# Residual rows of a hybrid layer: the store of h1 and h2 moved from right behind its accumulating DMA to a later step

## The chip, the cores and the metric

The kernel runs on one core of a Trainium2 chip. The metric is the device time of one execution in microseconds (us). Three runs of the kernel before took 2553.04, 2545.64 and 2548.37 us, a median of 2548.37 us.

## The reference

One layer of a transformer-like trunk over 2048 rows ("tokens") of 1024 float32 numbers:

```python
u = rms_norm(h, g_mix_pre[l]); z = u @ w_in[l]
ya = swa_with_sinks(...); yh = hgrn2(...)          # two head groups
y = jnp.concatenate([ya, yh], axis=-1) @ w_out[l]
h = h + rms_norm(y, g_mix_post[l])                 # h1
u = rms_norm(h, g_x_pre[l]); m = rms_norm(mem, g_mem[l])
y = cross_attention(u, m, wq_x[l], wk_x[l], wv_x[l], wo_x[l])
h = h + rms_norm(y, g_x_post[l])                   # h2
u = rms_norm(h, g_ffn_pre[l])
y = (jax.nn.silu(u @ w_gate[l]) * (u @ w_up[l])) @ w_down[l]
h = h + rms_norm(y, g_ffn_post[l])
```

The change concerns the two middle sums, h1 and h2: each is kept in DRAM for the sum that comes after it, and each is normalised at once for the product that follows.

## The kernel before

**Products.** Every float32 matrix is split into a high and a low part, and a product is three matmuls: high by high (line L1117), high by low (L1118), low by high (L1119). The high part comes from `split2` on ACT (L980, ScalarE) or POOL (L982, GpSimd), the low part on DVE (L983, VectorE). A split weight block is called T in the trace, a split block of activations S. Blocks of 2x2 are multiplied by a scheme with seven products (`seven`), whose sums of operands are formed on DVE (L1086).

**Stages around the change.** After the token mixing come, as steps of one long loop in `phases`: the out projection (`mixed_block`), the scores of cross attention (`score_block`), the values (`value_block`, whose weights hold the memory's values times the output matrix), and then the feed-forward blocks (`hidden_blocks`, `down_block`). A block of the first three works on two tiles of 128 rows, numbered n and n + 1; NT is 16, so each stage has eight blocks. A step is one of the seven products. After it `phases` advances every running generator by one `yield`: the `after()` of the blocks already computed, the splits and the loads of coming weights.

**After a block of the out projection.** `out` adds the partial products into a row tile y[i] (L1482 on DVE, L1484 on ACT) and has ACT square it (L1460). `after()` forms the inverse root of the mean square in three small POOL instructions (`rstds`, L1471 to L1475), scales the row (DVE, L1507), and starts on POOL a DMA that adds the input row onto it (`add`, L1489, an accumulating DMA). Right behind it stands the store of the row into `h1_d`. It is issued on SP (SyncE) and has to wait until the accumulating DMA has landed. Then `rest()` squares the finished row for the next norm (`mean_squares`, ACT, L1460), takes its `rstds`, transposes the row on PE (L1371) with copies on ACT (L1372), and stores it to `h1t_d`. Blocks n = 12 and 14 (n >= NT - 4) do not go on at once: their `rest()` is handed to the next stage and loads the row from DRAM again.

**After a block of the values** the same happens with `h2_d`: scaling at L1591, adding the row of `h1_d`, store into `h2_d`. Its `rest()` scales once more (L1612), transposes, stores to `u_d`, and for some blocks forms differences on DVE (L1627, L1628, L1631, L1632), stores them in quarters (`u_s0`) and first loads an earlier row of `u_d` for that purpose.

**What sets the order.** `load` (L75) and `store` (L78) both issue on SP, so they share one queue in which a waiting store holds up everything behind it. Row tiles come from one pool of nine (`row_tile`); who takes a tile next waits for the last reader of its earlier contents. The order of the instructions on each engine is not that of the text: a scheduler of the tile framework places them by a time simulation of its own. `with self.behind():` tells that scheduler that what follows may be placed only behind the last instructions of ACT, DVE, PE and SP that the step had; it adds no wait to the program.

Of the kernel before, what the change touches and what calls it, by code (L numbers as in the profile page):

```python
# [18 lines left out]
P = 128  # L19
# [10 lines left out]
NT = T // P  # L30
# [18 lines left out]
class Layer:  # L49
# [1441 lines left out]
    def mixed_block(self, n):  # L1491
        nc = self.nc
        y, ss = {}, []

        def out(i, j, a, b):
            if not y:
                ss.append(self.small("q_s", 4))
                if not n:
                    self.g_mix_post = self.gain(self.I["g_mix_post"])
            if i not in y:  # L1500
                y[i] = self.row_tile()
            self.squared(y[i][:, j * 512:(j + 1) * 512], a, b, ss[0][:, 2 * i + j:2 * i + j + 1])

        def after():
            r = self.rstds(ss[0])
            for i in range(2):
                nc.vector.scalar_tensor_tensor(y[i], y[i], r[:, i:i + 1], self.g_mix_post, ALU.mult, ALU.mult)  # L1507
                self.add(y[i], self.I["x"], n + i)
                self.store(self.h1_d[(n + i) * P:(n + i + 1) * P, :], y[i])
                yield  # L1510
            if n < NT - 4:
                yield
                yield from rest()

        def rest():
            s2 = self.small("q_s", 4)
            if n >= NT - 4:
                for i in range(2):
                    y[i] = self.rows_of(self.h1_d, n + i)
                for _ in range(3):  # L1520
                    yield
            for i in range(2):
                self.mean_squares(y[i], i, s2)
                yield
            r = self.rstds(s2)
            nc.gpsimd.tensor_scalar(self.r_x[:, n:n + 2], r, 1.0, None, ALU.mult)
            yield
            for i in range(2):
                self.store(self.h1t_d[n + i], self.transposed(y[i], y[i]))
                yield  # L1530

        if n >= NT - 4:
            self.rests[0].append(rest)

        return self.tokens(self.y_d, n), out, after, None

    def score_block(self, n):
# [35 lines left out]
    def value_block(self, n):  # L1573
        nc = self.nc
        y, ss = {}, []

        def out(i, j, a, b):
            if not y:
                ss.append(self.small("q_s", 4))
            if i not in y:  # L1580
                y[i] = self.row_tile()
                if n == 0 and len(y) == 1:
                    self.g_x_post = self.gain(self.I["g_x_post"])
                    self.g_ffn_pre = self.extra_tile()
                    self.load(self.g_ffn_pre, self.I["g_ffn_pre"][0:1, :].broadcast_to([P, D]))
            self.squared(y[i][:, j * 512:(j + 1) * 512], a, b, ss[0][:, 2 * i + j:2 * i + j + 1])

        def after():
            r = self.rstds(ss[0])
            for i in range(2):  # L1590
                nc.vector.scalar_tensor_tensor(y[i], y[i], r[:, i:i + 1], self.g_x_post, ALU.mult, ALU.mult)  # L1591
                self.add(y[i], self.h1_d, n + i)
                self.store(self.h2_d[(n + i) * P:(n + i + 1) * P, :], y[i])
                yield
            if n < NT - 4:
                yield
                yield from rest()

        def rest():
            s2 = self.small("q_s", 4)  # L1600
            if n >= NT - 4:
                for i in range(2):
                    y[i] = self.rows_of(self.h2_d, n + i)
                for _ in range(3):
                    yield
            for i in range(2):
                self.mean_squares(y[i], i, s2)
                yield
            r = self.rstds(s2)
            u = [self.row_tile() for _ in range(2)]  # L1610
            for i in range(2):
                nc.vector.scalar_tensor_tensor(u[i], y[i], r[:, i:i + 1], self.g_ffn_pre, ALU.mult, ALU.mult)  # L1612
                yield
            o = []
            yield
            for i in range(2):
                tv = self.transposed(u[i], u[i])
                self.store_transposed(self.u_d, n + i, tv)
                if 4 <= n < 8:
                    o.append(self.row_tile().rearrange("p (k t) -> p k t", k=KT))  # L1620
                    self.load(o[i], self.u_d[:, :, (n + i - 4) * P:(n + i - 3) * P].rearrange("k p t -> p k t"))
                yield
            for i in range(len(o)):
                tv = u[i].rearrange("p (k t) -> p k t", k=KT)
                s = self.row_tile().rearrange("p (k t) -> p k t", k=KT)
                with self.behind():
                    nc.vector.tensor_tensor(s[:, 0:4], tv[:, 0:4], o[i][:, 0:4], ALU.subtract)  # L1627
                    nc.vector.tensor_tensor(s[:, 4:8], tv[:, 4:8], tv[:, 0:4], ALU.subtract)  # L1628
                yield
                with self.behind():  # L1630
                    nc.vector.tensor_tensor(o[i][:, 0:4], o[i][:, 0:4], s[:, 4:8], ALU.add)  # L1631
                    nc.vector.tensor_tensor(o[i][:, 4:8], o[i][:, 4:8], o[i][:, 0:4], ALU.subtract)  # L1632
                at = slice((n + i - 4) * P, (n + i - 3) * P)
                for c, t in enumerate((s[:, 0:4], s[:, 4:8], o[i][:, 0:4], o[i][:, 4:8])):
                    self.store(self.u_s[c][:, :, at], t)
                yield

        if n >= NT - 4:
            self.rests[1].append(rest)
        return self.tokens(self.pt_d, n), out, after, None  # L1640

    def hidden_blocks(self, b, f):
# [139 lines left out]
```

## Time and profile before

| quantity | value |
|---|---|
| median of three runs | 2548.37 us |
| the profiled execution | 2551.66 us |
| its span, first to last instruction | 2549.9 us (1.76 us lie around it) |
| mean granted TensorE clock | 0.998 |
| busy: PE, DVE, ACT, POOL | 2506.9, 1760.8, 1250.6, 463.0 us |
| DMA issues of h_d<-row (h1 and h2) on SP | 32, 512 KB each, 7.2 us to landing |
| accumulating DMAs of these two stages on POOL | 16 from x, 16 of the 30 from h_d; all 74 of the kernel take 5.0 to 11.6 us, median 7.4 |

All numbers of the prediction come from this one execution. PE is TensorE, PEld its weight loads, SPq a queue's own time on SP. The trace leaves the buffer numbers out, so both h1_d and h2_d read h_d there, row is a tile of the pool of nine, q_s and q_r are the small sums and roots, junk is the output of a square that nobody reads. In a row of a timeline the first number is the start, the second the duration, both in us; "[1.95 <-DVE row L1612]" means that the engine was idle for 1.95 us and that this released it.

### The profile page before, as it was taken

The page shows a single profiled execution, that of the slowest core. Times are in us where ns is not written, and L with a number is a line of the kernel's source. Part 1 is how long each engine was busy: PE and PEld are TensorE (multiplying, and loading weights), DVE is VectorE, ACT ScalarE, POOL GpSimd, SP SyncE. Part 2 cuts the span into 40 slices and gives each one's busy share as a digit, 9 for nine tenths or more (in the row PEclk, how much of TensorE's full clock was granted, in tenths as well). Part 3 has the DMA queues.
Part 4 walks back from the last instruction along what each step waited for, and adds up shares of the span by engine and source line. Part 5 has one row for each costly group of instructions (what it writes and reads, how often), then busy time and mean ns, then how long its engine had stood idle before and what let it go on. Part 6 is the DMA issues. An engine that isn't in the chain of part 4 may idle for free.

```text
span 2549.9 us, 34114 instructions
## 1 busy us (share of the span) xinstructions
PE 2506.9 (98%) x12012; PEld 2089.9 (82%) x12012; DVE 1760.8 (69%) x2813; ACT 1250.6 (49%) x2606; POOL 463.0 (18%) x643
## 2 busy tenths in 40 slices
PE   8999999999999999999999999999999999999998
PEld 6777888887998888888788888888888888888786
DVE  6869487788667587787775655586566566664756
ACT  5454365656555566565554333353333344533543
POOL 2234243223422243233210000000000000000022
PEclk9999999999999999999999999999999999999999
DMA  6263544466887795859974542254555433667798
GB/s 239 95 219 128 174 141 157 152 202 212 282 308 223 216 283 195 282 185 254 297 232 133 178 144 79 95 182 146 182 195 194 158 128 134 205 206 200 218 225 207
DMA packets 269386, 489.97 MB, mean 192 GB/s; under 512 B 20640, under 2 KB 127136, under 8 KB 268704
## 3 DMA queue, kind: packets, MB, share of 16 engines
q1 hardware_dynamic: 255392, 438.52, 50.8%
q0 software_dynamic: 12672, 46.14, 8.9%
q10 hardware_dynamic: 1152, 3.15, 0.3%
q8 instruction: 94, 1.54, 0.2%
q14 instruction: 76, 0.62, 0.1%
HBM read 326.26 MB, written 161.48 MB: 191 GB/s over the span
## 4 chain that ended last, share of the span: by engine, by line
PE 87%; DMA 5%; DVE 3%; issue 2%; ACT 1%; POOL 1%; SPq 0%; DVEq 0%; POOLq 0%; ACTq 0%
PE psm L1117 23%; PE psm L1119 23%; PE psm L1118 23%; PE psg L172 3%; PE psg L170 3%; PE psg L171 3%; PE pss L1371 1%; DMA row<-h_d 1%; DMA row<-in_x_dram 1%; PE pss L830 0%; DMA qq<-z_d 0%; DVE S L983 0%; PE pst L830 0%; DMA z<-w_s 0%; DVE u L983 0%
## 5 line engine op out<-in xcount | busy, mean ns | idle before, releaser
L1117 PE MATMUL psm<-T,S 128*128 128x512 f32 x2744 | 1062.4, 391 | 8.4 <-ACT S L980 3.5
L1118 PE MATMUL psm<-T,S 128*128 128x512 f32 x2744 | 1070.3, 390 | 0.0
L1119 PE MATMUL psm<-T,S 128*128 128x512 f32 x2744 | 1063.5, 391 | 3.8 <-DVE S L983 3.6
L1117 PEld LDWEIGHTS psm<-T,S 128*128 128x128 f32 x2744 | 515.6, 188 | 119.6 <-ACT S L980 4.6
L1119 PEld LDWEIGHTS psm<-T,S 128*128 128x128 f32 x2744 | 515.5, 188 | 115.4 <-DVE S L983 8.0
L1118 PEld LDWEIGHTS psm<-T,S 128*128 128x128 f32 x2744 | 515.6, 188 | 106.4
L980 ACT ACTIVATE S<-sum 128x512 fp32r<-128x512 f32 (+1 forms) x336 | 206.1, 618 | 332.4 <-PE psm L1119 329.5
L983 DVE TENSOR_TENSOR S<-sraw,S 128x512 fp32r<-128x512 f32 (+1 forms) x312 | 211.3, 684 | 216.3 <-ACT S L980 196.4
L983 DVE TENSOR_TENSOR S<-sum,S 128x512 fp32r<-128x512 f32 (+1 forms) x400 | 271.8, 684 | 78.4 <-ACT S L980 61.2
L1132 ACT ACTIVATE part<-psm 128x512 f32<-128x512 f32 x294 | 173.3, 592 | 186.1 <-PE psm L1119 184.9
L980 ACT ACTIVATE S<-sraw 128x512 fp32r<-128x512 f32 (+1 forms) x271 | 165.9, 617 | 161.8 <-PE psm L1119 148.8
L1489 POOL DMA_DIRECT2D row<-y_d x28 | 25.0, 891 | 1071.2 <-DMA sraw<-hid_d 905.3
L172 PE MATMUL psg<-u,wlo 128*128 128x512 f32 x352 | 141.9, 403 | 4.6 <-DVE wlo L153 4.6
L1460 ACT ACTIVATE junk<-row 128x512 f32<-128x512 f32 x160 | 99.6, 624 | 93.6 <-DVE row L1482 32.4
L983 DVE TENSOR_TENSOR T<-row,T 128x1024 fp32r<-128x1024 f32 x104 | 123.7, 1198 | 30.1 <-ACT T L980 29.9
L170 PE MATMUL psg<-u,whi 128*128 128x512 f32 x352 | 142.1, 404 | 0.0
L171 PE MATMUL psg<-u,whi 128*128 128x512 f32 x352 | 141.8, 403 | 0.0
L980 ACT ACTIVATE T<-row 128x1024 fp32r<-128x1024 f32 x104 | 105.3, 1023 | 21.7 <-DMA row<-in_w_down_dram 8.6
L1664 DVE TENSOR_TENSOR part<-psm,part 128x512 f32<-128x512 f32 x66 | 45.4, 689 | 64.9 <-PE psm L1119 64.6
L1655 DVE TENSOR_TENSOR row<-psm,part 128x512 f32<-128x512 f32 x66 | 45.5, 689 | 57.1 <-PE psm L1119 57.0
L153 DVE TENSOR_TENSOR wlo<-raw,whi 128x1024 fp32r<-128x1024 f32 x54 | 68.1, 1263 | 23.8 <-ACT whi L150 11.9
L172 PEld LDWEIGHTS psg<-u,wlo 128*128 128x128 f32 x352 | 66.8, 190 | 19.3 <-DVE wlo L153 5.3
(343 smaller groups left out, 3450.2 us busy)
## 6 DMA issues: line engine op xcount, KB each, us to landing
sraw<-in_w_gate_dram SPq DMA_DIRECT2D x44, 512.0 KB, 4.9
sraw<-in_w_up_dram SPq DMA_DIRECT2D x44, 512.0 KB, 4.9
hid_d<-row SPq DMA_DIRECT2D x44, 512.0 KB, 2.7
h_d<-row SPq DMA_DIRECT2D x32, 512.0 KB, 7.2
y_d<-row SPq DMA_DIRECT2D x32, 512.0 KB, 3.9
sraw<-hid_d SPq DMA_DIRECT2D x32, 512.0 KB, 5.2
row<-h_d POOLq DMA_DIRECT2D x30, 512.0 KB, 7.2
row<-y_d POOLq DMA_DIRECT2D x28, 512.0 KB, 7.5
```

Of the source, the lines that this page charges most:

```text
L153: nc.vector.tensor_tensor(lo, raw, f32(hi), ALU.subtract)
L170: nc.tensor.matmul(ps, ah, bh, start=(i == 0), stop=False)
L171: nc.tensor.matmul(ps, ah, bl, start=False, stop=False)
L172: nc.tensor.matmul(ps, al, bh, start=False, stop=(i == n - 1))
L980: self.nc.scalar.activation(hi, raw, AF.Copy)
L983: self.nc.vector.tensor_tensor(lo, raw, f32(hi), ALU.subtract)
L1117: nc.tensor.matmul(ps, s[:, 0, k, :], t[:, 0, k, :], start=st, stop=False, **kw)
L1118: nc.tensor.matmul(ps, s[:, 0, k, :], t[:, 1, k, :], start=False, stop=False, **kw)
L1119: nc.tensor.matmul(ps, s[:, 1, k, :], t[:, 0, k, :], start=False, stop=sp, **kw)
L1132: nc.scalar.activation(t, ps, AF.Copy)
L1460: self.nc.scalar.activation(junk, a, AF.Square, scale=float(D) ** -0.5, accum_out=to)
L1655: nc.vector.tensor_tensor(d, a, c, ALU.add)
```

## The change

In both `after()` functions the store leaves the loop behind the accumulating DMA and becomes a function `keep()`, which stores both rows of the block under `behind()`. For n < 12 `rest()` calls it when both rows have been squared for the next norm and ahead of `rstds`. For n = 12 and 14 `after()` yields three times more and calls it then. This is the out projection; the values have the same edit with `h2_d`.

```diff
             for i in range(2):
                 nc.vector.scalar_tensor_tensor(y[i], y[i], r[:, i:i + 1], self.g_mix_post, ALU.mult, ALU.mult)
                 self.add(y[i], self.I["x"], n + i)
-                self.store(self.h1_d[(n + i) * P:(n + i + 1) * P, :], y[i])
                 yield
             if n < NT - 4:
                 yield
                 yield from rest()
+            else:
+                for _ in range(3):
+                    yield
+                keep()
+
+        def keep():
+            for i in range(2):
+                with self.behind():
+                    self.store(self.h1_d[(n + i) * P:(n + i + 1) * P, :], y[i])
...
             for i in range(2):
                 self.mean_squares(y[i], i, s2)
                 yield
+            if n < NT - 4:
+                keep()
             r = self.rstds(s2)
```

The scheduler makes of this less than the text suggests: 23 of the 32 stores keep their place in SP's queue. Three places where rows stand differently follow; the first number in a tile's name is the tile's, the second, which counts all names, shifts a little between the two kernels.

The first is SP at the end of the out projection. `h1t_d` takes transposed rows, `qk_d` and `qk_s` are the weights of the scores.

```order
L78 DMA h1t_d_59<-row_1257_9002 128x1024
L75 DMA row_1337_9363<-qk_d_63 128x2x512
L78 DMA h1_d_61<-row_1286_9133 128x1024
L75 DMA row_1348_9396<-qk_d_63 128x2x512
L75 DMA row_1355_9424<-qk_d_63 128x2x512
L75 DMA row_1364_9456<-qk_s_4508 128x1024
```

```order
L78 DMA h1t_d_59<-row_1257_9000 128x1024
L75 DMA row_1337_9361<-qk_d_63 128x2x512
L75 DMA row_1348_9394<-qk_d_63 128x2x512
L75 DMA row_1355_9422<-qk_d_63 128x2x512
L78 DMA h1_d_61<-row_1286_9132 128x1024
L75 DMA row_1364_9456<-qk_s_4508 128x1024
```

Of before and of the change in this order: the store of row_1286 has gone behind the two loads from `qk_d`.

The second is ACT a few microseconds later in the program, where it splits weights (T) and activations (S) into their high parts, before and then with the change.

```order
L980 ACTIVATE T_1329_9337<-row_1337_9363 128x1024
L1132 ACTIVATE part_1357_9439<-psm_1356_9426 128x512
L980 ACTIVATE S_1381_9549<-sum_1380_9547 128x512
L980 ACTIVATE T_1347_9395<-row_1348_9396 128x1024
L1132 ACTIVATE part_1365_9470<-psm_1318_9276 128x512
```

```order
L980 ACTIVATE T_1329_9335<-row_1337_9361 128x1024
L1132 ACTIVATE part_1357_9437<-psm_1356_9424 128x512
L980 ACTIVATE T_1347_9393<-row_1348_9394 128x1024
L980 ACTIVATE S_1381_9549<-sum_1380_9547 128x512
L1132 ACTIVATE part_1365_9470<-psm_1318_9276 128x512
```

The split of row_1348, which one of the two loads fills, has moved ahead of that of S_1381. On DVE the low parts of the two change places in the same way.

The third is SP towards the end of the values, before and then with the change.

```order
L78 DMA u_d_65<-row_1915_12147 128x8x128
L78 DMA h2_d_62<-row_1884_12004 128x1024
L78 DMA h2_d_62<-row_1904_12111 128x1024
L78 DMA u_s0_4512<-row_1935_12237 512x1x128
L78 DMA u_s0_4512<-row_1957_12351 512x1x128 x2
L78 DMA u_s0_4512<-row_1935_12237 512x1x128
L78 DMA u_s0_4512<-row_1942_12275 512x1x128
L75 DMA row_1984_12461<-u_d_65 128x8x128
```

```order
L78 DMA u_d_65<-row_1915_12147 128x8x128
L78 DMA u_s0_4512<-row_1935_12236 512x1x128
L78 DMA u_s0_4512<-row_1957_12349 512x1x128 x2
L78 DMA u_s0_4512<-row_1935_12236 512x1x128
L78 DMA h2_d_62<-row_1884_12003 128x1024
L78 DMA h2_d_62<-row_1904_12109 128x1024
L78 DMA u_s0_4512<-row_1942_12273 512x1x128
L75 DMA row_1984_12460<-u_d_65 128x8x128
```

The two stores to `h2_d` have gone behind four quarter stores to `u_s0`. In the same way those of row_1833 and row_1852 have gone behind the `u_d` stores of row_1867 and row_1868, and those of row_1929 and row_1950 behind quarter stores of row_1984 and row_2006. Behind the last row shown the order runs on alike in both: the load into row_1991, the load of a weight block, and the `u_d` store of row_1961.

More of the change, by code (lines that the diff above doesn't have):

```diff
@@ L1592, in after @@
                 self.add(y[i], self.h1_d, n + i)
-                self.store(self.h2_d[(n + i) * P:(n + i + 1) * P, :], y[i])
                 yield
@@ L1597, in after, with keep @@
                 yield from rest()
+            else:
+                for _ in range(3):
+                    yield
+                keep()
+        def keep():
+            for i in range(2):
+                with self.behind():
+                    self.store(self.h2_d[(n + i) * P:(n + i + 1) * P, :], y[i])
         def rest():
@@ L1608, in rest @@
                 yield
+            if n < NT - 4:
+                keep()
             r = self.rstds(s2)
```

## The prediction

> **What bounds the kernel now.** I read the page first, then the waits of TensorE (PE), a table of stretches, and the timelines round the stores. The page's first part gives busy time, share of the span and instructions; its fourth part gives the chain of work that ended last.
>
> ```profile
> PE 2506.9 (98%) x12012; PEld 2089.9 (82%) x12012; DVE 1760.8 (69%) x2813; ACT 1250.6 (49%) x2606; POOL 463.0 (18%) x643
> ...
> PE 87%; DMA 5%; DVE 3%; issue 2%; ACT 1%; POOL 1%; SPq 0%; DVEq 0%; POOLq 0%; ACTq 0%
> ```
>
> PE is busy for 2506.9 of 2549.9 us, so all its idle time together is 43 us. A change that only moves stores can take out no more than what PE idles where it acts. The instructions of all five engines stand in their old order up to the out projection, at about 740 us; on PE the order differs only in rows 4503 to 5139 of 11758, between about 840 and 1240 us. The next view gives PE's waits from 870 to 1270 us (total, times, longest), and the third the busy time of each engine by stretch (columns: length, PE, PEld, DVE, ACT, POOL, granted clock, share of the DMA engines).
>
> ```profile
> PE psm L1117 <- ACT S L980: 2.7, 1, 2.7
> PE pss L1371 <- DVE row L1612: 2.0, 1, 2.0
> PE psm L1119 <- DVE S L983: 0.8, 2, 0.6
> ```
>
> ```profile
> 870.00:960.00 90.00, 89.47 (x411) 73.00 (x410) 67.62 (x83) 57.14 (x120) 37.59 (x48) 1.00 0.87 267
> 900.00:910.00 10.00, 10.00 (x45) 8.28 (x45) 9.29 (x13) 3.79 (x11) 3.68 (x5) 1.00 1.01 263
> 960.00:1110.00 150.00, 150.00 (x727) 125.10 (x726) 119.11 (x214) 93.77 (x227) 40.89 (x58) 1.00 0.71 240
> 1110.00:1205.00 95.00, 94.56 (x456) 78.38 (x455) 72.67 (x102) 53.13 (x123) 33.94 (x43) 1.00 0.70 195
> 1205.00:1260.00 55.00, 49.73 (x228) 40.55 (x227) 40.86 (x54) 31.16 (x71) 18.44 (x26) 0.97 1.01 299
> ```
>
> Three stretches leave PE idle for 0.53, 0 and 0.44 us, and the fourth for 5.27 us at a granted clock of 0.97. So the out projection with its stores (870 to 960) and most of the values run at PE's own pace; only the end of the values does not. The stores themselves look dear on SyncE's queue (SP), in the view of that queue's waits:
>
> ```profile
> SPq L78 <- DMA row<-h_d: 133.9, 25, 17.4
> ...
> SPq L78 <- DMA row<-in_x_dram: 71.9, 16, 13.4
> ```
>
> SP stands 206 us behind accumulating DMAs, but PE pays almost nothing of it. What the change can give back is therefore not 206 us.
>
> **The change, part by part.** No instruction is added or dropped: 1042 DMAs on SP before and after, the same bytes, and no new kind of wait on the stores. It moves 32 stores. Of these, 13 of 16 to h1_d and 10 of 16 to h2_d keep their place in SP's queue, since the scheduler had put them late already; for those I count nothing. Nine move. All tile numbers below are those of the order. For row_1149, row_1378 and the pairs row_1833/1852 and row_1884/1904 SP's rows move, but what their engines then do shifts by less than the time by which it was early.
>
> *The out projection.* One store, that of row_1286, moves behind two loads of qk_d rows. SP's timeline, POOL's accumulate and what the DMA queues carried from 898 to 920 us (packets, MB, share of 16 engines' time; the last row has a load's us to landing):
>
> ```profile
> 899.88 0.39 SPq L75 DMA_DIRECT2D row<-qk_d  x1
> 908.65 0.32 SPq L78 DMA_DIRECT2D h_d<-row  x1
> 909.07 1.25 SPq L75 DMA_DIRECT2D row<-qk_d  x2
> ```
>
> ```profile
> 902.26 0.94 POOL L1489 DMA_DIRECT2D row<-in_x_dram  x1 [1.68 <-DMA sraw<-h1t_d]
> ```
>
> ```profile
> q1 hardware_dynamic: 2023, 5.48, 71.7%
> q0 software_dynamic: 288, 1.05, 25.8%
> ...
> row<-qk_d SPq DMA_DIRECT2D x3, 512.0 KB, 6.1
> ```
>
> SP idles from 900.27 to 908.65 for the accumulate issued at 902.26, and the two loads leave at 909.07. Now they can leave at about 900.3 and are there some 8 us earlier. Nothing on PE wanted them here. What it does instead is change the order on ACT and DVE: the split of row_1348 (T) now stands ahead of that of S_1381. ACT, DVE and PE at that place before:
>
> ```profile
> 908.74 0.63 ACT L1460 ACTIVATE junk<-row 128x512 f32<-128x512 f32 x1 [0.15 <-DMA row<-in_x_dram]
> ...
> 911.41 0.62 ACT L1460 ACTIVATE junk<-row 128x512 f32<-128x512 f32 x1
> ...
> 914.06 0.62 ACT L980 ACTIVATE S<-sum 128x512 fp32r<-128x512 f32 x1
> 914.90 1.06 ACT L980 ACTIVATE T<-row 128x1024 fp32r<-128x1024 f32 x1 [0.22 <-DMA row<-qk_d]
> ```
>
> ```profile
> 913.72 1.22 DVE L983 TENSOR_TENSOR T<-row,T 128x1024 fp32r<-128x1024 f32 x1 [1.43 <-ACT T L980]
> 914.86 0.68 DVE L983 TENSOR_TENSOR S<-sum,S 128x512 fp32r<-128x512 f32 x1
> ```
>
> ```profile
> 914.79 0.45 PE L1117 MATMUL psm<-T,S 128*128 128x512 f32 x1
> 915.07 0.40 PE L1118 MATMUL psm<-T,S 128*128 128x512 f32 x1
> 915.60 0.50 PE L1119 MATMUL psm<-T,S 128*128 128x512 f32 x1
> ```
>
> S_1381's high half ends at 914.68, and PE takes it at 914.79: 0.11 us to spare. Its low half starts on DVE at 914.86 and PE takes it at 915.60, with none to spare. Now T goes first: ACT 914.06 to 915.12, DVE from 915.15, and one such T holds DVE for 914.86 - 913.72 = 1.14, so the low half starts at 916.29 instead of 914.86. PE stops for **1.4 us** more (the high half, at 1.06 - 0.11 = 0.95, is hidden in this). It ends at 0 from below: the rows leave ACT 0.22 and 0.15 us of idle time to win, and S cannot come earlier than it did with T ahead of it.
>
> To this comes a delay Δ of the chain that feeds ACT. It starts from the accumulate of row_1286, at 908.74 with no slack, and the two loads now run beside it in DMA engines that are full (share 1.01 from 900 to 910). By the queue rows a load of 0.52 MB takes 0.717 x 352 / 5.48 x 0.52 / 16 = 1.5 us of the sixteen engines (352 is 16 times 22 us), so both take 3.0: Δ lies between 0 and 3.0. The packets take 0.315 us on q0 (0.258 x 352 / 288) and 0.125 on q1. Up to about 906 (899.88 + 6.1) SP's older load is under way in both kernels; if packets of the two queues alternate in the 2.6 us after that, the accumulate lands 2.6 x 0.125 / 0.315 = **1.0 us** later, which I take. The Trainium skill, "DMA: Bandwidth & Descriptors", section "Queues, rings and completion order", says that each DMA engine takes turns between the queue rows packet by packet; by that rule it is this 1.0, and a first-come rule would make it nearer 3.0. The rows of this trace do not show which.
>
> Together 2.4 us. Of the idle 0.53 us in 870 to 960 some 0.2 goes in return, so **+2.2 us** here.
>
> *The end of the values.* PE, DVE, ACT and the chain of waits there:
>
> ```profile
> 1236.19 1.06 PE L1371 MATMUL pss<-ident,row 128*128 128x128 f32 x8 [1.95 <-DVE row L1612]
> ...
> 1254.73 0.50 PE L1117 MATMUL psm<-T,S 128*128 128x512 f32 x1 [2.71 <-ACT S L980]
> ...
> 1256.08 0.80 PE L1119 MATMUL psm<-T,S 128*128 128x512 f32 x1 [0.61 <-DVE S L983]
> ```
>
> ```profile
> 1231.18 0.69 DVE L1627 TENSOR_TENSOR row<-row,row 128x512 f32<-128x512 f32 x1 [5.81 <-DMA u_d<-row]
> ```
>
> ```profile
> 1251.40 0.63 ACT L1460 ACTIVATE junk<-row 128x512 f32<-128x512 f32 x1 [2.87 <-DMA row<-h_d]
> ```
>
> ```profile
> 1243.14 8.15 DMA row<-h_d
> ```
>
> ```profile
> 1255.50:1259.00 3.50, 2.92 (x7) 2.37 (x8) 2.28 (x3) 3.50 (x7) 2.24 (x4) 0.51 0.98 285
> ```
>
> PE waits 1.95 + 2.71 + 0.61 = 5.27 us. The granted clock then falls to 0.51 for 3.5 us, in which half the work is lost: 1.7 us. So this end costs 7.0 us. The chain is: DVE idle for 5.81 us until the store of row_1961 to u_d has landed, then busy without a break up to the two scalings ahead of the accumulates (the first issued at 1243.14, landing after 8.15), then ACT's squares at 1251.40, behind which S stands. The DMA engines are full all along (1.01). The nine moved stores change which transfer stands first in a full queue, not how much is in it: ahead of the u_d store of row_1961 stands the same set as before. So I count **0**. From below, the u_d stores of row_1867/1868 no longer wait behind the h2_d stores,
>
> ```profile
> 1179.65 6.46 SPq L78 DMA_DIRECT2D h_d<-row  x2
> ```
>
> and can leave about 4 us before 1186.1; if all of that came through, the 7.0 would go. From above, see the second rival.
>
> The clock decides whether 2.4 us at S_1381 stay 2.4. In this trace a stop of 1.95 cost no clock and one of 2.71 followed by 0.61 did. With Δ = 3.0 the stop is 4.4 us and would bring 1.7 more; with my value I count none. The Trainium skill, "TensorE: Matmul & The Clock Gate", section "Why this matters for your kernels", puts the danger at idle gaps over some 3 us; the row at 2.71 shows that a gap a little under it with another behind it does it too, so by the rule nothing is lost here and by the row nearly.
>
> **Sum:** 1.4 + 1.0 - 0.2 + 0 = +2.2 us on the profiled execution of 2551.66, which lies 3.3 above the median of the three runs, 2548.37. Measured against that median: 2550.5.
>
> **Rivals.** *The end of the values heals.* The 7.0 us go, since the u_d stores leave earlier; with +2.2 that gives 2543.6, and 2541.4 if the stop at S_1381 fails too. For it: SP stood still for 6.46 us ahead of them. Against it: the queue is full, and an accumulate that runs beside these stores lands later. Chance 0.2.
>
> *A store that goes later holds a row tile.* There are nine tiles for rows, and whoever takes a tile next waits for the store that still reads it. In the new order the load into row_1991 takes the tile of row_1884, whose store has gone behind four u_s0 stores. Rows of SP, and the landing of that store before (last number):
>
> ```profile
> 1203.12 4.62 SPq L78 DMA_DIRECT2D h_d<-row  x2
> ...
> 1216.14 0.77 SPq L75 DMA_DIRECT2D row<-u_d  x1
> ```
>
> ```profile
> h_d<-row SPq DMA_DIRECT2D x1, 512.0 KB, 9.4
> ```
>
> The store landed at 1203.12 + 9.4 = 1212.5. Four quarter-megabyte stores ahead of it (0.262 MB each at the 299 GB/s of the window) take 3.5 us, so it lands at 1216.0, and the load wants the tile at 1216.14. It decides from a landing after 1216.1: then SP stops with the u_d store of row_1961 two transfers behind it, which is the one DVE waits for. Spread over the 9.4 us a delay of 4 us is possible, and a second place of the same make follows at the load into row_2039: 4 + 4 + 2.2 = +10.2, 2558.6. Against it: a full DMA queue hides an issuer that stops for a moment. Chance 0.16.
>
> *The change does not do what it says.* 23 of 32 stores keep their place, and if the low half of S_1381 is in time anyway, the time stays: 2548.4. Chance 0.22.
>
> **How the numbers follow.** The forecast, +2.2 with Δ from 0 to 3.0 and the clock (+1.2 to +5.9), has 0.42. The range 2543 to 2558 takes in that, the idle third rival, most of the first and most of the second. A measurement of this kernel tells 0.3% (7.6 us) from no change. Faster than 2540.7 needs all 7.0 us of the end and more: 0.06, of the first rival. Slower than 2556.0 needs most of the second, or Δ with the clock and part of it: 0.13. The rest, 0.81, is no change.
>
> **What would show it.** Right: the two qk_d loads at about 900.3 on SP, the T split ahead of S at 914 to 915 on ACT, and a stop of 2 to 3 us on PE there; the accumulate of row_1286 landing about a microsecond after 908.7; the three waits of PE near 1236 to 1256 still there, within a microsecond or two. Wrong: no stop near 915 (the order of ACT costs nothing), a missing wait on u_d at 1231 (first rival), or SP waiting in front of a row load for an h2_d landing near 1216 or 1241 (second rival).

## The result, and the profile after

The changed kernel takes 2558.28 us (median of 6 runs, 2557.64 to 2561.21); the kernel before, run beside it, 2548.62 us (6 runs). The ratio is 1.0033, with a 95% interval of 1.0023 to 1.0042: 5.9 to 10.7 us slower. The sign is the one forecast (+2.2 us), the size is about four times that, and the time lies 0.28 us above the upper end of the range. The changed kernel's profiled execution took 2558.54 us, with a span of 2556.7 us against 2549.9.

The waits of PE (TensorE) from 870 to 1270 us in the changed kernel (total, times, longest), the counterpart of the first such view of before:

```profile
PE psm L1117 <- ACT S L980: 6.0, 2, 3.4
PE psm L1117 <- ACT part L1132: 3.2, 4, 1.3
PE pss L1371 <- DVE row L1632: 1.2, 1, 1.2
PE psm L1119 <- DVE S L983: 0.6, 1, 0.6
PE pss L1371 <- DMA row<-in_x_dram: 0.5, 1, 0.5
```

And its busy time by stretch, where the changed kernel loses against before (the columns are those of the prediction's table; PE was busy for 89.47 us of 870 to 960 there):

```profile
870.00:960.00 90.00, 85.92 (x389) 70.10 (x388) 63.98 (x79) 54.52 (x113) 34.26 (x46) 0.98 0.82 243
919.00:923.00 4.00, 3.35 (x8) 2.63 (x9) 3.85 (x4) 4.00 (x9) 0.57 (x1) 0.60 0.65 219
960.00:1110.00 150.00, 148.70 (x720) 123.83 (x719) 116.44 (x210) 89.92 (x221) 44.20 (x59) 1.00 0.74 249
```

The old wait for S at the end of the values is still there (2.6 of the 6.0 us). New is a wait for S of 3.4 us, with the clock at half speed behind it, and that is the place the prediction named. PE's own timeline has it as the second of three stops:

```profile
912.40 1.06 PE L1371 MATMUL pss<-ident,row 128*128 128x128 f32 x8 [0.48 <-DMA row<-in_x_dram]
...
919.65 0.69 PE L1117 MATMUL psm<-T,S 128*128 128x512 f32 x1 [3.44 <-ACT S L980]
...
964.54 0.47 PE L1117 MATMUL psm<-T,S 128*128 128x512 f32 x1 [1.30 <-ACT part L1132]
```

Upstream the two executions had drifted apart by 0.6 us, so this matmul at 919.65, which began at 914.79 before, is 4.2 us later by its own place. ACT (ScalarE) says why. Its rows in the changed kernel:

```profile
912.37 0.63 ACT L1460 ACTIVATE junk<-row 128x512 f32<-128x512 f32 x1 [3.18 <-DMA row<-in_x_dram]
...
915.37 0.63 ACT L1460 ACTIVATE junk<-row 128x512 f32<-128x512 f32 x1 [0.24 <-DMA row<-in_x_dram]
...
918.04 1.04 ACT L980 ACTIVATE T<-row 128x1024 fp32r<-128x1024 f32 x1
918.98 0.61 ACT L980 ACTIVATE S<-sum 128x512 fp32r<-128x512 f32 x1
```

The square that started at 908.74 before starts at 912.37, 3.0 us later than the drift, and waits for the accumulating DMA itself. T stands ahead of S, as the order had shown, and holds ACT for 0.94. SP (SyncE) sends the three loads of qk_d in one go, as forecast, and then stands still for the accumulate:

```profile
900.48 2.23 SPq L75 DMA_DIRECT2D row<-qk_d  x3
912.28 0.33 SPq L78 DMA_DIRECT2D h_d<-row  x1
```

The accumulates land later. The DMA issues of the out projection, 800 to 960 us (KB each, median us to landing), and then the accumulate of row_1286 by itself, each of before and then of the changed kernel:

```profile
row<-in_x_dram POOLq DMA_DIRECT2D x16, 512.0 KB, 7.2
```

```profile
row<-in_x_dram POOLq DMA_DIRECT2D x16, 512.0 KB, 9.2
```

```profile
row<-in_x_dram POOLq DMA_DIRECT2D x1, 512.0 KB, 6.4
```

```profile
row<-in_x_dram POOLq DMA_DIRECT2D x1, 512.0 KB, 9.4
```

The accumulate of row_1286 went from 6.38 us to 9.40, that of row_1300 from 7.66 to 11.23. The median is not the doing of the two loads alone: the accumulates of blocks 12 and 14 are later too (the last 13.55 us against 11.52), and in a run below whose out projection stands as before (values without block 4) the last took 13.14. SP's waiting, which the change attacks, hardly fell: in the changed kernel it stands 127.5 + 73.7 = 201 us behind accumulating DMAs, 206 before. Of the 206 us, 86 lie behind 1400 us, where the change moves nothing; in the two stages themselves the wait fell from 119 to 113 us.

```profile
SPq L78 <- DMA row<-h_d: 127.5, 22, 17.7
...
SPq L78 <- DMA row<-in_x_dram: 73.7, 16, 13.8
```

### The profile page after: what moved, and what is told of

It reads as the page before. It is cut to its first block, busy times and chain, and to the rows that moved or that the text cites. A ratio compares the mean times of both kernels' runs of the same rounds, so it can differ in the third digit from the quotient of the medians.

```text
span 2556.7 us, 34111 instructions
## 1 busy us (share of the span) xinstructions
PE 2509.4 (98%) x12012; PEld 2092.9 (82%) x12012; DVE 1760.3 (69%) x2813; ACT 1249.7 (49%) x2606; POOL 464.3 (18%) x643
## 4 chain that ended last, share of the span: by engine, by line
PE 86%; DMA 5%; DVE 3%; issue 3%; ACT 2%; POOL 1%; SPq 0%; DVEq 0%; POOLq 0%; ACTq 0%
PE psm L1117 22%; PE psm L1119 22%; PE psm L1118 22%; PE psg L172 3%; PE psg L170 3%; PE psg L171 3%; PE pss L1371 1%; DMA row<-in_x_dram 1%; DMA row<-h_d 1%; ACT junk L1460 1%; PE pss L830 1%; DVE S L983 1%; PE pst L830 0%; DMA qq<-z_d 0%; DVE u L983 0%
## 5 line engine op out<-in xcount | busy, mean ns | idle before, releaser
L980 ACT ACTIVATE T<-row 128x1024 fp32r<-128x1024 f32 x104 | 105.2, 1023 | 19.9 <-DMA row<-in_w_down_dram 9.8
L982 POOL TENSOR_SCALAR S<-sum 128x512 fp32r<-128x512 f32 x64 | 51.8, 809 | 172.5 <-PE psm L1119 142.7
```

The costliest lines, as they stand in the source:

```text
L980: self.nc.scalar.activation(hi, raw, AF.Copy)
L982: self.nc.gpsimd.tensor_scalar(hi, raw, 1.0, 1.0, ALU.mult, ALU.mult)
```

## The experiments

**The theory** after these profiles (A): two loads that no longer wait behind a store run beside an accumulating DMA, which then lands 3 us later; ACT, and PE with it, wait for that, the T split ahead of S adds a microsecond, and the half clock the rest. The rivals: the values' half carries the loss (B); the order on ACT is the cause and the late accumulate is hidden (D). For each kernel the length of a stretch between the same two matmuls, 870 to 985 us (out projection, start of the scores) and 1205 to 1275 us (end of the values) of before, is given beside the time, since one execution differs from the next by 2 us and more upstream of all this. Differences in us are taken from the ratio of the runs, with its 95% interval.

```
kernel                      870-985   1205-1275   ratio to before (95%)
before                       115.11       69.94
before, second profile       114.27       68.57
the change                   121.66       70.89   1.0033 (1.0023 to 1.0042)
out projection's half        121.45       69.09   1.0022 (1.0011 to 1.0033)
values' half                 115.90       70.91   1.0013 (1.0004 to 1.0022)
values' half, once more      114.44       71.25   1.0008 (0.9999 to 1.0018)
change, block 10 as before   114.91       69.60   1.0012 (1.0003 to 1.0020)
change, S ahead of T         119.81       69.17   1.0023 (1.0012 to 1.0035)
values without block 4       115.19       68.05   0.9999 (0.9990 to 1.0008)
values, block 4 alone        114.05       69.47   1.0001 (0.9993 to 1.0010)
stores on ACT's queue        128.29       67.97   1.0078 (1.0064 to 1.0092)
```

**The out projection's half alone.** `mixed_block` as changed, `value_block` as before.

> Only the out projection's half of the change; the values are as before. Theory A (the stop at S_1381 is the cause: two loads beside the accumulate of row_1286 land it 3.0 us later, the T split ahead of S adds 1.0, half clock adds 1.7, and a later stop at 964 adds 1.1): about 2548.6 + 6.7 = 2555.3 us, with a stop of some 3.4 us near 919. Rival B (the end of the values, where a store of n = 4 goes into a full queue, carries most): about 2549 to 2550, the stop near 919 harmless.

2555.83 us against 2549.86, +5.7 us (2.8 to 8.4). The stop stands at 916.64 with 3.29 us, the accumulate of row_1286 takes 9.63 us, and the stretch is 6.3 us longer than in the first profile of before. Theory A's 6.7 lies inside; B does not hold for the greater part.

**The values' half alone, twice.**

> Only the values' half. Theory A: 2549 to 2550.5 us, no stop near 915, a new wait of DVE for a u_d store of about 2.4 us near 1207 and a PE stop of 1.3 us behind it, partly given back at the transposes near 1236. Rival B: 2554 to 2556.

> The values' half alone once more, since neither of its parts alone moved the time. Theory I (the two parts cost only together, at the u_d store of row_1914 and the landings behind it): again 2 to 5 us slower than before. Theory J (the first figure of 3.3 us was mostly spread between runs): within 0.1% of before, as each part was, so that nearly all of the change's loss is the out projection's.

+3.3 us (1.0 to 5.6), then +2.0 (-0.3 to 4.6). No stop over a microsecond near 915. The first figure lies above theory A's time and below B's; the second fits both I and J and does not decide between them. So this half is probably not free, though the prediction counted nothing for it; what of it can be placed follows below.

**The one block put back.** In the whole change, the stores of block n = 10 of the out projection stand right behind their accumulates again:

```diff
                 self.add(y[i], self.I["x"], n + i)
+                if n == 10:
+                    self.store(self.h1_d[(n + i) * P:(n + i + 1) * P, :], y[i])
                 yield
...
-            if n < NT - 4:
+            if n < NT - 4 and n != 10:
                 keep()
```

> The whole change, but for the one block n = 10 of the out projection, whose two stores stand right behind their accumulating DMAs as before, so that the two qk_d loads go out behind the store of row_1286. Theory A: like the values alone, 2549 to 2550.5 us, ACT and DVE split S_1381 ahead of T again, the accumulate of row_1286 lands after 6.4 us. If the other moved stores of the out projection matter (rival C): 2552 or more.

2552.63 us against 2549.86: +3.1 us (0.8 to 5.1), like the values' half. The accumulate of row_1286 takes 6.25 us, and on ACT S is back ahead of T, which waits for its load as it did before:

```profile
907.84 0.63 ACT L1460 ACTIVATE junk<-row 128x512 f32<-128x512 f32 x1 [0.32 <-DMA row<-in_x_dram]
...
913.16 0.62 ACT L980 ACTIVATE S<-sum 128x512 fp32r<-128x512 f32 x1
914.65 1.06 ACT L980 ACTIVATE T<-row 128x1024 fp32r<-128x1024 f32 x1 [0.86 <-DMA row<-qk_d]
```

The stretch is 114.91, as before. The time lies where rival C was put (2552 or more), but that line was drawn for a values' half that costs nothing; beside the values' half alone (+3.3 and +2.0 us) no loss is left. So of the sixteen stores of h1 one pair carries what the runs can tell of the out projection's loss, and C falls within their spread of some 2 us.

**The order mended, the loads still early.** In the whole change an edge for the scheduler puts the split of row_1348 behind that of S_1381 on ACT and DVE (it adds no wait; `first_split` holds the instructions of the split of row_1348, the lines that record them are not shown):

```diff
             self.split2(src, t[:, 0], t[:, 1], engine or e)
+            if self._n == 1381:
+                for i in self.first_split:
+                    s = next(x for x in traced[m:] if x.engine == i.engine)
+                    self.tc.add_manual_dep(i, s.name, mybir.DependencyInfo(
+                        mybir.DependencyClass.NoSync, mybir.DependencyReason.DATA), reason="issue_after")
```

> The whole change, with the split of row_1348 ordered behind that of S_1381 on ACT and DVE as before, while the two qk_d loads still go out early. Theory A: contention stays and the order is mended: the accumulate of row_1286 still takes 9.4 us, the stop shrinks from 3.4 to about 2.5 us, 2557.3 us with the half clock and 2555.6 without. Rival D (the order is the cause, the later accumulate is hidden): stop under 0.5 us, about 2551.

2555.69 us, +5.9 us (3.1 to 8.9). ACT and PE there (the lines are 11 higher in this kernel):

```profile
917.75 0.62 ACT L980 ACTIVATE S<-sum 128x512 fp32r<-128x512 f32 x1
918.27 1.05 ACT L980 ACTIVATE T<-row 128x1024 fp32r<-128x1024 f32 x1
```

```profile
918.42 0.57 PE L1128 MATMUL psm<-T,S 128*128 128x512 f32 x1 [2.65 <-ACT S L980]
```

The accumulate still takes 9.66 us and the stop is 2.65: forecast 2.5. Half clock follows it, for which 2557.3 us had been forecast. The stop at 964 is gone as well, because the mended order also brings back, 40 us on, a copy of a partial product ahead of two exponentials on ACT. By the stretches, 114.91 without both, 119.81 with the late accumulate, 121.66 with both: the late accumulate costs about 4.9 us, half clock included, and the order, with the stop at 964, about 1.9. The second is a rough figure: the seven profiles in which the store of row_1286 stands in its old place spread over 1.9 us here (114.05 to 115.90), and the intervals of the two ratios overlap. D falls.

**The accumulates by themselves.** A kernel of DMAs alone, with nothing of the layer computed: groups of loads on SP beside accumulating DMAs on POOL (GpSimd).

> DMAs alone, nothing of the layer computed: groups of zero to four loads of 512 KB (2 KB pieces, issued on SP) beside one or two accumulating DMAs of 512 KB (issued on POOL), each group behind the end of the one before, three times over. Theory A1 (the two queues take turns, so a load beside delays an accumulate by about the load's own time on the engines): two accumulates land 1.2 to 1.6 us later for each load beside them, about 3 us for two loads. Theory A2 (an accumulate's pieces only let one short piece of a load in between, ratio 0.125 to 0.315): about 1 us for two loads and no more for four. Rival D (accumulates are not slowed by loads): under 0.3 us.

The median landing of two accumulates, with none, two, three and four loads of 512 KB beside them (one group each, from the first of three rounds):

```profile
big<-in_x_dram POOLq DMA_DIRECT2D x2, 512.0 KB, 6.3
...
big<-in_w_dram SPq DMA_DIRECT2D x2, 512.0 KB, 4.6
big<-in_x_dram POOLq DMA_DIRECT2D x2, 512.0 KB, 9.1
...
big<-in_w_dram SPq DMA_DIRECT2D x3, 512.0 KB, 5.1
big<-in_x_dram POOLq DMA_DIRECT2D x2, 512.0 KB, 9.8
...
big<-in_w_dram SPq DMA_DIRECT2D x4, 512.0 KB, 8.2
big<-in_x_dram POOLq DMA_DIRECT2D x2, 512.0 KB, 9.7
```

Over the three rounds the first of two accumulates takes 5.4 to 5.7 us alone, 7.8 to 8.1 beside two loads, 8.2 to 8.4 beside three or four (beside a single load 6.56, 6.01 and 8.06). The second takes 7.3 to 7.6 alone, 9.8 to 10.0 beside two and 11.0 to 11.1 beside three or four. The first two loads are hardly delayed in return: they land after 3.9 to 4.2 and 5.0 to 5.3 us, against 3.7 to 4.0 and 4.7 to 4.9 with no accumulate there. A third load lands after 11.2 us, about when the second accumulate does. What the queues carry beside three loads shows how (packets, MB, share of 16 engines' time; q0 has the accumulates, q1 the loads), from 95 to 98.9 us and then from 100 to 105 us:

```profile
q1 hardware_dynamic: 483, 0.96, 85.7%
```

```profile
q0 software_dynamic: 209, 0.79, 79.2%
q1 hardware_dynamic: 210, 0.43, 25.4%
```

First only loads run: the first packet of the accumulate issued at 94.71 stands 4.3 us behind its issue, against 1.6 to 1.7 us alone. Then the two queues alternate packet by packet, 209 to 210 in these 5 us and 36 to 51 beside 36 to 52 in each single one. So the first two loads go ahead whole, at 1.2 us each; the third takes turns with the accumulates, which makes the second of them another 1.2 us later and the load itself more than 5 us later (5.5 to 5.7 us with no accumulate there). That is A1 for the loads that go ahead and A2's turns for the rest; why just two go ahead is not shown. The Trainium skill, "DMA: Bandwidth & Descriptors", section "Queues, rings and completion order", gives the turn as a whole packet of some 9 to 17 descriptors. A load of 512 KB in 2 KB pieces is 256 pieces over 16 engines, 16 for each; the rows from 100 to 105 us show turns of one such piece, so here the page's count does not fit, and the measurement decides.

**A second profile of before.**

> The kernel before once more, for a second profile beside the first: the length of the stretches of PE that no store touches tells how far one execution differs from another. If the stretch of the values (1110 to 1275 us) differs by more than 0.9 us between the two, the values' half cannot be priced from one profile each.

From 1110 to 1275 us the two executions differ by 1.41 us (164.83 and 163.42). One profile each cannot price the values' half.

**What the values' half costs, in two parts.** The stores of block n = 4 put back, and those alone moved:

```diff
                 self.add(y[i], self.h1_d, n + i)
+                if n == 4:
+                    self.store(self.h2_d[(n + i) * P:(n + i + 1) * P, :], y[i])
                 yield
...
```

This is put into the values' half, where `keep()` then passes over block 4 (not shown); the other kernel is the one before with `keep()` for block 4 alone.

> The values' half alone, but with the two stores of block n = 4 (row_1833, row_1852) right behind their accumulating DMAs as before. Theory E (those two, pushed behind the u_d stores of row_1867 and row_1868 into a full queue, delay the u_d store of row_1914 by about 1.1 us and so what DVE does next): the time goes back to within 1 us of before, 2550 to 2551, and the u_d store of row_1914 goes out at 1193.8 again. Rival F (the values' half costs by the other four stores, or by nothing that its order shows): 2552.5 to 2554 as with the whole half.

> The kernel before, with only the two stores of block n = 4 of the values (row_1833, row_1852) moved behind the u_d stores of row_1867 and row_1868; every other row of SP stands as before. Theory E (this pair carries the values' half): 1 to 3 us slower than before, the u_d store of row_1914 out about a microsecond later than before by the order of its stretch. Rival F (the half's cost came from the other stores, or was spread of the runs): within 1 us of before.

Neither moves the time: -0.3 us (-2.6 to 2.0) and +0.3 (-1.8 to 2.5). The u_d store of row_1914 does as theory E has it, at 1194.12 us with the pair in its old place and at 1195.25 with the pair moved (1193.75 before). The profiles do sort by that pair. Where it stands in its old place (both of before, the out projection's half, the half without block 4) the end of the values takes 68.05 to 69.94 us, mean 68.9; where it has moved (six profiles) 69.17 to 71.25, mean 70.2. In five of those six PE has a stop near 1219 (0.16 to 1.31 us) that the other four lack; the changed kernel's row:

```profile
1227.01 0.50 PE L1117 MATMUL psm<-T,S 128*128 128x512 f32 x1 [1.31 <-ACT part L1132]
```

With the pair moved the accumulate of row_1904 takes 10.1 to 11.6 us, else 9.1 to 9.4. So some 1.3 us of the values' half go with that pair, and with an accumulate that lands later. This is a difference of means of ranges that overlap, so the place is likely and not shown. The mean of the two runs of the whole half is about 2.7 us, and the two parts add up to nothing; whether the rest is the parts acting together or the spread of the runs stays open.

**The waits taken off SP.** The whole change, with the 32 stores on ACT's queue:

```diff
                 with self.behind():
-                    self.store(self.h1_d[(n + i) * P:(n + i + 1) * P, :], y[i])
+                    self.put(self.h1_d[(n + i) * P:(n + i + 1) * P, :], y[i])
... (the same for h2_d)
```

> The whole change, with the 32 stores issued on ACT's queue instead of SP's, so that SP never waits for an accumulating DMA. Theory A (that wait kept loads away from the accumulates, and taking it away makes them land later): slower than before, 2555 to 2562, with a stop of 2 us or more near 915 and accumulates of the out projection that take more than 7.4 us in the median. Rival G (SP's 206 us of waiting are what the kernel should save): faster than before, 2545 or less.

2572.16 us against 2552.56: +19.9 us (16.3 to 23.5), further than theory A went. Accumulates of the out projection take 9.7 us in the median, that of row_1286 10.83, and PE stops six times from 870 to 970 us (its waits there):

```profile
PE psm L1117 <- ACT part L1132: 3.4, 1, 3.4
PE pss L1371 <- DMA row<-in_x_dram: 2.9, 2, 2.1
PE psm L1119 <- DVE S L983: 2.9, 2, 2.5
PE psm L1117 <- ACT S L980: 2.2, 1, 2.2
```

The last two of the six stops have another cause than loads beside an accumulate. The stores of blocks 12 and 14 now stand in ACT's own order, ahead of splits and copies, and wait there for their accumulates, so ACT stands still in SP's place. The rows of ACT that release these two stops, and PE's:

```profile
959.44 0.63 ACT L980 ACTIVATE S<-sum 128x512 fp32r<-128x512 f32 x1 [3.48 <-DMA row<-in_x_dram]
963.50 0.60 ACT L1132 ACTIVATE part<-psm 128x512 f32<-128x512 f32 x1 [3.43 <-DMA row<-in_x_dram]
```

```profile
960.12 0.50 PE L1117 MATMUL psm<-T,S 128*128 128x512 f32 x1 [2.19 <-ACT S L980]
964.25 0.77 PE L1117 MATMUL psm<-T,S 128*128 128x512 f32 x1 [3.39 <-ACT part L1132]
```

Of the loss 13.2 us lie in the first stretch, and 7.9 between 1275 and 1400 us (133.06 against 125.16). The second has the same cause: ACT stands 3.22 and 3.54 us behind accumulates of h2 there, and PE stops for 2.32 and 3.40. These four stops are 11.3 us of the loss, ahead of any half clock. So SP's wait for the accumulates of the two stages (119 us before, 6.6 here) was not taken away but put on an engine that computes. Theory A's sign came, and the accumulates did land later, but this run cannot part the two causes, and it does not refute G: what the kernel would save if nothing stood in SP's place is not tested.

**A way on.** If an accumulate is what loads disturb, fewer of them should help. From the kernel before: the rows of h1 are loaded ahead and added on DVE, in blocks 10, or 8 and 10, of the values.

```diff
+            h = [self.rows_of(self.h1_d, n + i) for i in range(2)] if n in BY_DVE else None
...
-                self.add(y[i], self.h1_d, n + i)
+                if n in BY_DVE:
+                    nc.vector.tensor_tensor(y[i], y[i], h[i], ALU.add)
+                else:
+                    self.add(y[i], self.h1_d, n + i)
```

> A way on from the kernel before: in block n = 10 of the values the rows of h1 are loaded ahead into two row tiles and added on DVE, in place of the two accumulating DMAs. Theory A (a late accumulate costs PE the 2.6 + 0.5 us near 1255 and the half clock behind it; a load takes about 1.25 us of the DMA engines where an accumulate takes 2): the stop near 1255 goes, 3 to 5 us faster than before. Rival H (the stop is set by DVE and ACT in that stretch, and two tiles of nine taken early make others wait): no gain or slower.

> The same for the blocks n = 8 and n = 10. Theory A: the stop near 1236 shrinks as well, since the u_d store of row_1961 no longer shares the engines with two accumulates: 4 to 6 us faster than before. Rival H: four tiles taken early cost more than they give, slower than with block 10 alone.

With block 10 alone 2550.86 against 2550.49, no change (1.0002, 0.9993 to 1.0012) where 3 to 5 us were expected, though its profile has a stop of 1.55 us in place of the 2.71 + 0.61 and no half clock behind it. That profile is of the fastest of its executions, 2546.85 us, so it may show more than the median holds. With both blocks 2547.04 us, ratio 0.9986 (0.9977 to 0.9994): 1.5 to 5.9 us faster than the kernel before, where 4 to 6 were expected, and the best version seen. Its waits of PE from 870 to 1400 us and its end of the values, where before had 49.73 us of PE and a clock of 0.97:

```profile
PE psm L1120 <- DVE S L984: 1.2, 2, 0.7
PE psm L1118 <- ACT S L981: 0.7, 1, 0.7
PE psm L1118 <- ACT part L1133: 0.4, 1, 0.4
```

```profile
1205.00:1260.00 55.00, 54.18 (x254) 44.27 (x253) 49.37 (x63) 32.56 (x75) 18.27 (x23) 1.00 1.04 340
```

PE gains 4.45 us here, and DVE works 8.5 us more; the measured gain of 3.6 is of that size. The 2 us of the DMA engines that the expectation put on an accumulate were too few: in the kernel of DMAs alone two accumulates with no load beside them land 2.4 to 2.6 us apart.

## Why the prediction was right in sign and short in size

**The bound** held: PE is busy for 98% of the span in both kernels, and the parts of the span outside the two stretches agree within about 1 us.

**That SP's 206 us are not to be had** held for this change, which took 5 us of the wait away and lost time. Whether some of it could be had otherwise is open, since the one run that emptied SP's queue put the wait on ACT.

**The place and the mechanism** held: loads at 900.5, T ahead of S, a stop of PE at S_1381. The step that failed is the size of Δ, "if packets of the two queues alternate in the 2.6 us after that, the accumulate lands 1.0 us later, which I take". It landed 3.0 us later, the upper bound given. The turns were not the error but where they begin: the accumulate does not start as before and then share. Its first packet stands 4.55 us behind its issue, 1.63 before, so 2.9 of the 3.0 us pass ahead of it, while the queues carry loads and stores of SP alone (902.8 to 907 us of the changed kernel):

```profile
q1 hardware_dynamic: 632, 1.40, 100.7%
```

Then the queues do take turns, 135 packets of accumulates to 117 of SP's from 909 to 912 us, and the second of the two moved loads lands 12.3 us behind its issue. With that bound the text itself had a stop of 4.4 us and 1.7 for the clock; the profile has 0.48 + 3.44 = 3.9 us of stops, 4.2 against the drift, and about 1.7 lost to the clock. That the 2.4 us forecast would have cost no clock was not safe either: single stops of 2.37 us and up lost it in other runs (last section).

**The low half of S_1381** was argued wrongly. PE does not wait for it: twelve matmuls of another S stand between the high half's products and it in the new order, and no wait on DVE is there. The stop is the high half's, 3.02 for the late accumulate and about 0.9 for T. The 1.4 came out too large by some 0.5 us.

**"Some 0.2 goes in return"** was wrong: instead a stop of 1.30 at 964.5 came (0.19 was there before), from another swap on ACT. In all, the stretch from 870 to 985 us grew by 6.55 us against the first profile of before, where 2.2 were forecast.

**Nothing for the values** was probably too low. The rival of the row tile was not what happened: the load into row_1991 left behind the landing of the store that it waits for (1224.56 and 1223.40 in the changed kernel), so the tile was free in time. Shown is a u_d store of row_1914 that DVE waits for, 2.41 us, and a stop of 1.31 behind it, part of which comes back at the transposes (1.17 in place of 1.95). The first rival, that the u_d stores leave earlier, came true for the store of row_1867 alone, 4.7 us earlier; that of row_1868 waits for its transpose and gained nothing.

**The sum** as the runs leave it: 6.6 us in the out projection's stretch (roughly 3.9 of stops, 1.7 of clock, 1.1 at 964) and about 1.3 at the end of the values, together 7.9 of the 8.4 that the ratio gives; the rest has no place. The range's upper end, 2558.0, was made from the row tile's rival at both of its places, which did not happen. It nearly held the time because Δ at its bound with the clock, which the text priced at +5.9, met two small terms of the same sign. That the time came so near to the range was luck.

## What to carry to other kernels

A queue that stands still behind a transfer also keeps the transfers behind it out of that transfer's way; before taking such a wait away, look at what will run in its place, and at who waits for the slow one. A wait that is put on the queue of a computing engine, as the stores were on ACT's, holds up that engine's work too. Where a bound lies three times above the value taken, and the row beneath it has no slack, price the outcome at the bound. A difference of 0.1% needs more than one profile of each kernel: here executions of the same kernel differed by 1.4 us in a stretch of 165.

## What the runs showed of the hardware

A 512 KB accumulating DMA takes 5.2 to 5.7 us alone. Of a pair the first takes up to 8.4 us and the second up to 11.1 beside loads. The first two loads queued ahead land 0.1 to 0.3 us later in the median in return; a third shares the engines with the pair packet by packet and lands after 11.2 us.

Half clock came behind single stops of 3.44, 2.65 and 2.37 us (the change; S ahead of T; the values' half) and behind 2.19 followed by 0.61 (S ahead of T), while 2.51 followed by 0.61 (values without block 4) and single stops of 2.48 (stores on ACT's queue) and 1.95 (before) went without. So no one length between 2 and 2.7 us decides. The traces show what does. Half clock lasts 3.41 us or a multiple of it, and inside one profile its starts lie whole multiples of 3.41 us apart (919.80 and 1264.54 in the changed kernel: 101 of them). If the span is cut into stretches of 3.41 us on that grid, the clock fell at the end of every stretch at full clock in which PE idled for 1.91 us or more, and of none in which it idled for 1.87 or less: 36 falls in 9133 stretches between 30 and 2530 us, over the thirteen profiles of the layer. The 2.51 us of the values without block 4 lay across an edge of that grid, 1.87 us on one side. The Trainium skill, "TensorE: Matmul & The Clock Gate", section "What's actually happening", says that the window in which idling is counted runs freely and is 3413 ns long, and these rows agree. Its table asks for an idle window of some 3.4 us; here 1.91 us of idling inside one were enough, and the measurement decides.
